# Low parts of the context stream's weight pieces: from GpSimd to VectorE

## Chip, cores and metric

The kernel runs on one core of one Trainium2 chip. The metric is device time in microseconds (us) of one launch. A core has five engines that run side by side, each through its own instructions in a fixed order: TensorE (PE, with weight loads as PEld), VectorE (DVE), ScalarE (ACT), GpSimd (POOL) and SyncE (SP, which here only issues DMAs).

## The reference

Two blocks follow each other. The first runs on 256 tokens of x: two token mixers side by side, then a gated FFN. One of the mixers is a recurrence over the tokens. The second block has two layers on x and on 256 context tokens: half FFNs, three mixers, and shifts, scales and gates that come from a large product with `w_ada`. All data are float32.

```
def first_block(x, ...):
    xn = rms_norm(h, norm_mix[l])
    proj = xn @ w_in[l]
    y_r = rwkv7_group(proj[..., :R_COLS], ...)
    y_n = nsa_group(proj[..., R_COLS:], ...)
    h = h + jnp.concatenate([y_r, y_n], axis=-1) @ w_out[l]
    h = h + swiglu(rms_norm(h, norm_ffn[l]), ...)
# in rwkv7_group, one step per token:
    sa = jnp.einsum('bhvk,bhk->bhv', state, an_t)
    state = state * w_t[:, :, None, :] + sa[..., None] * b_t[:, :, None, :] + v_t[..., None] * k_t[:, :, None, :]
# second block
def _half_ffn(h, g, shift, scale, gate, w_up, w_down):
    return h + 0.5 * gate * _swiglu(_modulate(_rmsnorm(h, g), shift, scale), w_up, w_down)
mod_x = (jax.nn.silu(c) @ w_ada[l] + b_ada[l]).reshape(bn, 1, N_MOD, d)
h_c = _half_ffn(h_c, norm_g[l, 0], mod_c[:, :, 0], mod_c[:, :, 1], mod_c[:, :, 2], ffn1_up[l], ffn1_down[l])
```

## The kernel before

A float32 matrix product is made of three matmuls in a reduced float32 format. Weights and activations are each split into a high part, which is the value rounded to that format, and a low part, which is the rest. `gemm` (lines 360 to 366) runs high by high (line 364), low activation by high weight (365), and high activation by low weight (366). A weight piece of 128 x 1024 elements is brought by one DMA of 512 KB (line 349). ScalarE rounds it to its high part (line 356), and then another engine subtracts that from the piece, which leaves the low part (line 357). Such a piece feeds 24 matmuls of 256 columns.

`Stream` holds the buffers of such pieces and the engine that subtracts, `self.e`. There are three streams. `s1` and `s` carry the weights of x and subtract on VectorE. `sc` carries the weights of the context (the words "context stream" below) and is made with `eng=g`, so that its subtractions run on GpSimd. It has three buffers for raw pieces and two each for high and low parts. Through it go the 66 pieces of the context's first half FFN (44 up, 22 down) and the 14 pieces of the context's projections in layer 0, 80 in all; pieces of `w_ada` pass its raw buffers without a split.

The program is written as a sequence of pieces, and a scheduler decides in which order each engine's instructions stand; what an instruction is thought to take is the scheduler's own estimate. So a change of the engine for one kind of instruction can move others. Every engine then runs its list in order.

Around the change the first block and the context's first half FFN run interleaved. The first block's tile names on PE and DVE are those of block1: `P`, `sm` and `nm` are its attention, `lw`, `cum`, `kk`, `rk` the start of the recurrence (from line 823). Then come the Gram products (line 946), and a triangular solve in 31 steps on VectorE (`tm` and `TW`, lines 972 and 973), whose result goes through DRAM and back by DMAs (lines 975 and 979) into `TT`. The scan over 8 chunks follows: lines 989 to 1002 prepare it, and a chunk is line 1018 on PE, 1019 on DVE (`U`), 1021, 1026 and 1027 on PE, 1036 on DVE (`SB`), with 1035 on POOL. Its end goes over a norm with a power on POOL (line 850) to the last products 1078 and 1079. After that PE takes the first block's output projection (tile `m`, line 364 with `mixh`) and its FFN. The context FFN's matmuls have tiles `f` with `yhc`, `ylc` (up) and `hh`, `hl` (down); line 1163 are the `w_ada` matmuls. The context's next norm sums squares on POOL (line 398, tile `sa`), then on PE (388), and spreads its factor by line 421.

Of the kernel before, what the change touches and what calls it, by code (L numbers as in the profile page):

```python
# [15 lines left out]
OP = mybir.AluOpType  # L16
# [249 lines left out]
def build(tc, A, O, dbg=(), stop=None):  # L266
    nc = tc.nc
    v, s, g, te, sy = nc.vector, nc.scalar, nc.gpsimd, nc.tensor, nc.sync
    es = ExitStack()

    def pool(name, bufs=1, space=None, side=None, stack=es, **k):
        if space is not None:
            k["space"] = space
        if side is not None:
            k["side"] = side
        return stack.enter_context(tc.tile_pool(name=name, bufs=bufs, **k))
# [7 lines left out]
    def tl(p, shape, dt=F32, tag="", bufs=None, name=None):  # L284
        k = {}
        if tag:
            k["tag"] = tag
        if bufs:
            k["bufs"] = bufs
        return p.tile(list(shape), dt, name=uniq(name or tag or "t"), **k)  # L290
# [8 lines left out]
    f32 = lambda a: a.bitcast(F32)  # L299
# [31 lines left out]


    class Stream:
        def __init__(self, name, nr, nh, side=None, stack=es, eng=None, parts=None):
            self.nr = nr
            self.raw = pool(name + "r", nr, side=side, stack=stack)
            self.h = pool(name + "h", nh, side=side, stack=parts or stack)
            self.l = pool(name + "l", nh, side=side, stack=parts or stack)
            self.q = sy
            self.e = eng or v  # L340

        def load(self, src, a, b, i=0):

# [8 lines left out]
        def get(self, src, a, b):  # L352
            r = self.load(src, a, b)
            h = tl(self.h, [128, 1024], F32R, tag="h")[:, 0:a * b].rearrange("p (a b) -> p a b", a=a)
            l = tl(self.l, [128, 1024], F32R, tag="l")[:, 0:a * b].rearrange("p (a b) -> p a b", a=a)
            s.copy(h, r)  # L356
            self.e.tensor_tensor(l, r, f32(h), op=OP.subtract)  # L357
            return h, l

    def gemm(pt, w, m0, m1, xs):  # L360
# [1218 lines left out]
    R = "right"  # L1579
# [4 lines left out]

    rs, rs2 = ExitStack(), ExitStack()
    pad = pool("pada", 1, side=R, stack=rs)
    st_c = Stream("sc", 3, 2, side=R, stack=rs, eng=g, parts=rs2)
    st_c.pad = pad
    e = ExitStack()
    first = []  # L1590
# [89 lines left out]
    rs = ExitStack()  # L1680
# [75 lines left out]
```

## Time and profile before

| | before |
|---|---|
| median of 3 runs | 2326.54 us (2321.26 to 2328.99) |
| the profiled execution's own time | 2326.68 us |
| its span, first to last instruction | 2324.7 us |
| mean granted TensorE clock | 0.977 |
| PE busy | 2226.8 us, 96% of the span |
| PEld busy | 1943.0 us, 84% |
| DVE busy | 1367.7 us, 59% |
| ACT busy | 944.8 us, 41% |
| POOL busy | 367.5 us, 16% |

The span is the time between the first and the last instruction of that execution; the run's own time is some 2 us longer. PE's busy time is made of matmuls whose ends overlap, so a busy PE may still be waiting between small matmuls. The granted clock is the share of 2.4 GHz that TensorE got: it is either 1.0 or 0.5 at any moment, and a row shows its mean.

### The profile page before, as it was taken

To read this page: it belongs to the slowest core of one execution; us is meant where nothing else is said; L and a number is where in the kernel's file an instruction comes from. 1 tells how busy PE (TensorE), PEld (TensorE's weight loads), DVE (VectorE), ACT (ScalarE), POOL (GpSimd) and SP (SyncE) were. 2 spreads that over 40 slices of the span, in tenths; PEclk is the share of its full clock that TensorE was granted. 3 is DMA by queue.
4 is the path that set the end of the run, shared out by engine and by line. 5 is a ranking of instruction groups with operands and counts; after the bars stand their busy time and mean duration, and the time that the engine had idled before them with its cause. 6 is when DMAs were issued, how large, how long until landed. Compare 5 with 4: busy or idle time off the path is not lost.

```text
span 2324.7 us, 38368 instructions
## 1 busy us (share of the span) xinstructions
PE 2226.8 (96%) x15317; PEld 1943.0 (84%) x15317; DVE 1367.7 (59%) x2442; ACT 944.8 (41%) x1602; POOL 367.5 (16%) x286
## 2 busy tenths in 40 slices
PE   7999987999999899998999999999999999999998
PEld 3688876888999799997878777789988889878998
DVE  4555567348665776677765333357534347885665
ACT  4334431225444454445643222235322225574443
POOL 2124543455110300002010000011000001410000
PEclk9999988999999899999999999999999999999999
DMA  7865434336554234544166434465522234413553
GB/s 294 277 231 182 176 135 139 124 118 243 191 182 172 100 127 167 183 172 145 55 227 227 161 129 162 146 227 199 200 97 95 96 110 166 150 57 114 187 184 129
DMA packets 114929, 376.25 MB, mean 162 GB/s; under 512 B 18464, under 2 KB 24480, under 8 KB 114752
## 3 DMA queue, kind: packets, MB, share of 16 engines
q1 hardware_dynamic: 114752, 373.82, 46.4%
q8 instruction: 120, 1.97, 0.3%
q14 instruction: 57, 0.47, 0.1%
HBM read 372.20 MB, written 1.57 MB: 161 GB/s over the span
## 4 chain that ended last, share of the span: by engine, by line
PE 76%; issue 11%; DVE 7%; DMA 3%; POOL 2%; ACT 1%; SPq 0%; POOLq 0%; DVEq 0%; ACTq 0%
PE m L364 13%; PE m L366 13%; PE m L365 13%; PE f L364 7%; PE f L366 7%; PE f L365 7%; PE f L1163 4%; PE o L1391 2%; POOL sa L398 1%; DMA r<-in_ada 1%; PE f L1381 1%; DVE l L357 1%; DVE tm L972 1%; ACT h L356 1%; DMA r<-in_up 1%
## 5 line engine op out<-in xcount | busy, mean ns | idle before, releaser
L356 ACT CAST h<-r 128x1024 fp32r<-128x1024 f32 (+1 forms) x547 | 567.0, 1042 | 1050.3 <-PE m L365 426.2
L357 DVE TENSOR_TENSOR l<-r,h 128x1024 fp32r<-128x1024 f32 (+1 forms) x467 | 572.0, 1228 | 351.8 <-ACT h L356 342.3
L364 PE MATMUL m<-yh,h 128*128 128x256 f32 (+1 forms) x1624 | 489.5, 303 | 2.3 <-ACT h L356 1.1
L366 PE MATMUL m<-yh,l 128*128 128x256 f32 (+1 forms) x1624 | 489.1, 302 | 0.4 <-DVE l L357 0.4
L365 PE MATMUL m<-yl,h 128*128 128x256 f32 (+1 forms) x1624 | 489.5, 302 | 0.0
L364 PEld LDWEIGHTS m<-yh,h 128*128 128x128 f32 x1624 | 310.0, 191 | 25.8 <-ACT h L356 8.9
L366 PEld LDWEIGHTS m<-yh,l 128*128 128x128 f32 x1624 | 310.4, 191 | 18.2 <-issue 7.1
L365 PEld LDWEIGHTS m<-yl,h 128*128 128x128 f32 x1624 | 310.6, 191 | 15.4 <-issue 3.7
L357 POOL TENSOR_TENSOR l<-r,h 128x1024 fp32r<-128x1024 f32 x80 | 193.4, 2419 | 335.2 <-ACT h L356 327.7
L398 POOL TENSOR_TENSOR sa<-sa,sq 128x256 f32<-128x256 f32 x81 | 86.2, 1064 | 907.3 <-ACT sq L394 490.0
L365 PE MATMUL m<-hl,h 128*128 128x256 f32 (+1 forms) x738 | 220.1, 302 | 0.0
L366 PE MATMUL m<-hh,l 128*128 128x256 f32 (+1 forms) x738 | 219.9, 303 | 0.0
L364 PE MATMUL m<-hh,h 128*128 128x256 f32 (+1 forms) x738 | 215.5, 304 | 0.2
L364 PE MATMUL f<-yh,h 128*128 128x256 f32 (+1 forms) x624 | 199.6, 320 | 1.8 <-ACT yh L434 1.1
L365 PE MATMUL f<-yl,h 128*128 128x256 f32 (+1 forms) x624 | 198.0, 317 | 1.2 <-DVE yl L435 1.2
L366 PE MATMUL f<-yh,l 128*128 128x256 f32 (+1 forms) x624 | 197.9, 318 | 0.0
L364 PE MATMUL f<-hh,h 128*128 128x256 f32 (+1 forms) x446 | 138.5, 316 | 13.8 <-DVE ft L461 6.5
L366 PEld LDWEIGHTS m<-hh,l 128*128 128x128 f32 x738 | 139.1, 189 | 8.4 <-issue 1.6
L365 PEld LDWEIGHTS m<-hl,h 128*128 128x128 f32 x738 | 139.8, 190 | 6.7 <-issue 0.4
L364 PEld LDWEIGHTS m<-hh,h 128*128 128x128 f32 x738 | 136.3, 189 | 10.0 <-issue 2.1
L1541 DVE SCALAR_TENSOR_TENSOR res<-m,mod,res 128x256 f32<-128x256 f32 x176 | 79.1, 478 | 105.5 <-PE m L366 105.0
L365 PE MATMUL f<-hl,h 128*128 128x256 f32 (+1 forms) x446 | 136.8, 309 | 0.3 <-DVE hl L370 0.3
(513 smaller groups left out, 4079.6 us busy)
## 6 DMA issues: line engine op xcount, KB each, us to landing
r<-in_up SPq DMA_DIRECT2D x252, 512.0 KB, 3.6
r<-in_ada SPq DMA_DIRECT2D x144, 512.0 KB, 4.4
r<-in_dn SPq DMA_DIRECT2D x98, 512.0 KB, 3.8
r<-in_w1u SPq DMA_DIRECT2D x44, 512.0 KB, 3.5
r<-in_dn SPq DMA_DIRECT2D x32, 448.0 KB, 3.3
r<-in_w2m SPq DMA_DIRECT2D x24, 512.0 KB, 4.1
r<-in_w2o SPq DMA_DIRECT2D x24, 512.0 KB, 3.5
r<-in_w1d SPq DMA_DIRECT2D x22, 512.0 KB, 3.5
```

What stands on the lines that cost most here:

```text
L356: s.copy(h, r)
L357: self.e.tensor_tensor(l, r, f32(h), op=OP.subtract)
L364: te.matmul(pt, w[0][:, k, m0:m1], xs[k][0], start=k == 0, stop=False)
L365: te.matmul(pt, w[0][:, k, m0:m1], xs[k][1], start=False, stop=False)
L366: te.matmul(pt, w[1][:, k, m0:m1], xs[k][0], start=False, stop=k == n - 1)
L398: g.tensor_tensor(acc, acc, sq, op=OP.add)
L972: v.tensor_mul(tm, TW[:, 0:m, j:j + 1].to_broadcast([128, m, n]), Ls[:, j:j + 1, j + 1:32].to_broadcast([128, m, n]))
L1163: te.matmul(pt[j * 32:j * 32 + 32], adac[:, k], w[j], start=k == 0, stop=k == KD - 1)
L1381: te.transpose(pT[:, b * 128:b * 128 + 128], P[:, b * 128:b * 128 + 128], ident)
L1391: te.matmul(po[j * 64:j * 64 + 64], vals(b // 2, b % 2, kvof(2 * pr + j)), PT[j][:, b], start=b == 0, stop=b == nt - 1)
L1541: v.scalar_tensor_tensor(r, pt[:, i * T:i * T + T], ad[l].M[:, m, d, q:q + 1], r, op0=OP.mult, op1=OP.add)
```

## The change

The subtraction for the context stream's pieces goes to VectorE, with the same operands. The choice of an engine is taken out of `Stream`.

```diff
     class Stream:
-        def __init__(self, name, nr, nh, side=None, stack=es, eng=None, parts=None):
+        def __init__(self, name, nr, nh, side=None, stack=es, parts=None):
             self.nr = nr
             self.raw = pool(name + "r", nr, side=side, stack=stack)
             self.h = pool(name + "h", nh, side=side, stack=parts or stack)
             self.l = pool(name + "l", nh, side=side, stack=parts or stack)
             self.q = sy
-            self.e = eng or v
...
             s.copy(h, r)
-            self.e.tensor_tensor(l, r, f32(h), op=OP.subtract)
+            v.tensor_sub(l, r, f32(h))
             return h, l
...
-    st_c = Stream("sc", 3, 2, side=R, stack=rs, eng=g, parts=rs2)
+    st_c = Stream("sc", 3, 2, side=R, stack=rs, parts=rs2)
```

The file is one line shorter above line 356, so that a line of before is one lower in the changed kernel (356 is 355, 357 is 356, and so on). The scheduler puts the engines' lists into another order. Three places follow. Numbers behind the tiles' names tell buffers apart.

First PE, in the scan over chunks: the rows of one chunk from line 1018 on, and what stands behind its first product of line 1026. Tiles `f` are the context FFN. Before:

```order
L1018 MATMUL m_2514<-SB_406_1913,WT_2290 32x128 x4
L1021 MATMUL o_2463<-AR_2009,SB_406_1913 128x32 x4
L1026 MATMUL m_2524<-Vt_2078,Kt_2064 128x128
L364 MATMUL f_4895<-hh_4562,h_4877 128x256
L365 MATMUL f_4895<-hl_4563,h_4877 128x256
L366 MATMUL f_4895<-hh_4562,l_4878 128x256
```

Now:

```order
L1017 MATMUL m_2489<-SB_407_1914,WT_2290 32x128 x4
L1020 MATMUL o_2463<-AR_2009,SB_407_1914 128x32 x4
L1025 MATMUL m_2499<-Vt_2078,Kt_2064 128x128
L1026 MATMUL m_2499<-U_2334,Bt_2050 128x128
L1025 MATMUL m_2499<-Vt_2078,Kt_2064 128x128
L1026 MATMUL m_2499<-U_2334,Bt_2050 128x128
```

The context FFN's matmuls, 14 of them at this place, are gone from between the first product and the one that reads `U`; in the changed order none stands anywhere in the scan.

Second PE, at the end of the recurrence, around its last products. Before:

```order
L364 MATMUL f_5143<-hh_5011,h_5139 128x256
L1078 MATMUL m_2629<-gl_29_144,lora_2609 128x256
L1079 MATMUL m_2629<-gl_30_145,lora_2611 128x256
L1078 MATMUL m_2635<-gl_29_144,lora_2609 128x256
L1079 MATMUL m_2635<-gl_30_145,lora_2611 128x256
L365 MATMUL f_5143<-hl_5012,h_5139 128x256
```

Now:

```order
L1077 MATMUL m_2635<-gl_29_144,lora_2609 128x256
L1078 MATMUL m_2635<-gl_30_145,lora_2611 128x256
L387 MATMUL f_8025<-ones_67,sa_8026 128x1 x2
L420 MATMUL f_8056<-sq_8053,ones_67 128x256
L363 MATMUL m_5260<-mixh_147,h_5256 128x256
L364 MATMUL m_5260<-mixl_148,h_5256 128x256
L363 MATMUL f_8104<-yhc_8019,h_8100 128x256
```

The context FFN was still running there; now it is over, and the sums of the context's next norm (387 and 420) stand between the recurrence and the output projection.

Third DVE, in the triangular solve. Before:

```order
L972 TENSOR_TENSOR tm_2247<-TW_2181,Ls_2178 128x11x11
L973 TENSOR_TENSOR TW_2181<-TW_2181,tm_2247 128x11x11
L972 TENSOR_TENSOR tm_2250<-TW_2181,Ls_2178 128x11x10
L973 TENSOR_TENSOR TW_2181<-TW_2181,tm_2250 128x11x10
L972 TENSOR_TENSOR tm_2253<-TW_2181,Ls_2178 128x12x9
```

Now, with the pieces' low parts among the steps:

```order
L971 TENSOR_TENSOR tm_2205<-TW_2181,Ls_2178 128x4x25
L356 TENSOR_TENSOR l_4738<-r_4735,h_4737 128x1024
L972 TENSOR_TENSOR TW_2181<-TW_2181,tm_2205 128x4x25
L369 TENSOR_TENSOR hl_4720<-ft_4717,hh_4719 128x256
L971 TENSOR_TENSOR tm_2208<-TW_2181,Ls_2178 128x4x24
L972 TENSOR_TENSOR TW_2181<-TW_2181,tm_2208 128x4x24
L971 TENSOR_TENSOR tm_2211<-TW_2181,Ls_2178 128x5x23
L972 TENSOR_TENSOR TW_2181<-TW_2181,tm_2211 128x5x23
L356 TENSOR_TENSOR l_4810<-r_4807,h_4809 128x1024
```

The subtractions stand inside the chain that each next step reads.

## Rows read from the trace of the kernel before

**Rows 1.** The cores' view: span and mean granted clock.

```profile
core 0: 2324.7 us, clock 0.977
```

**Rows 2.** Windows: stretch, length, busy us (and instructions) per engine, clock, DMA share, GB/s.

```profile
118.00:287.80 169.80, 164.97 (x1303) 136.38 (x1302) 92.73 (x214) 72.40 (x160) 70.75 (x35) 0.99 0.54 193
287.80:363.30 75.50, 68.66 (x417) 53.64 (x416) 47.57 (x84) 20.71 (x31) 34.69 (x16) 0.91 0.42 143
363.30:414.10 50.80, 37.31 (x256) 32.52 (x255) 36.11 (x82) 11.67 (x15) 21.32 (x9) 0.87 0.45 138
414.10:522.50 108.40, 106.88 (x847) 92.33 (x846) 43.40 (x69) 25.98 (x40) 47.97 (x32) 0.97 0.34 119
522.50:569.00 46.50, 43.44 (x332) 39.08 (x332) 39.50 (x81) 26.13 (x44) 26.43 (x25) 0.96 0.80 278
793.00:814.00 21.00, 13.24 (x48) 10.86 (x48) 14.84 (x41) 9.48 (x25) 8.71 (x11) 0.51 0.07 26
2150.00:2200.00 50.00, 50.00 (x427) 50.00 (x426) 32.53 (x49) 21.62 (x28) 0.00 (x0) 1.00 0.53 182
```

**Rows 3.** Costliest groups of the page, line 357: busy, mean ns, idle before and releaser.

```profile
L357 DVE TENSOR_TENSOR l<-r,h 128x1024 fp32r<-128x1024 f32 (+1 forms) x467 | 572.0, 1228 | 351.8 <-ACT h L356 342.3
L357 POOL TENSOR_TENSOR l<-r,h 128x1024 fp32r<-128x1024 f32 x80 | 193.4, 2419 | 335.2 <-ACT h L356 327.7
```

**Rows 4.** Timeline of DVE in the solve: start us, us taken, instruction.

```profile
366.14 0.19 DVE L972 TENSOR_TENSOR tm<-TW,Ls 128x31 f32<-128x31 f32 x1 [1.85 <-DMA TW<-in_cst]
...
373.14 0.28 DVE L973 TENSOR_TENSOR TW<-TW,tm 128x115 f32<-128x115 f32 x1
373.46 2.43 DVE L972 TENSOR_TENSOR tm<-TW,Ls 128x110 f32<-128x110 f32 x1
...
403.69 0.19 DVE L973 TENSOR_TENSOR TW<-TW,tm 128x16 f32<-128x16 f32 x1
```

**Rows 5.** Timeline of POOL at the same time.

```profile
373.41 2.35 POOL L357 TENSOR_TENSOR l<-r,h 128x1024 fp32r<-128x1024 f32 x1 [4.60 <-ACT h L356]
```

**Rows 6.** Groups by line from 128 to 569 us.

```profile
L370 DVE TENSOR_TENSOR hl<-ft,hh 128x256 fp32r<-128x256 f32 x22 | 33.3, 1513 | 7.6 <-ACT hh L369 7.5
L398 POOL TENSOR_TENSOR sa<-sa,sq 128x256 f32<-128x256 f32 x14 | 14.7, 1053 | 15.6 <-ACT sq L394 14.6 <-DMA pw<-in_poolw 0.6
```

**Rows 7.** Waits of PE from 118 to 414 us: total, times, longest.

```profile
PE f L364 <- DVE ft L461: 6.5, 1, 6.5
PE f L364 <- DVE res L1541: 5.1, 4, 3.3
PE m L886 <- DVE rk L882: 4.3, 1, 4.3
...
PE f L364 <- DVE fu L457: 1.8, 1, 1.8
```

**Rows 8.** Timeline of PE in one chunk of the scan (filler left out).

```profile
442.38 1.04 PE L1018 MATMUL m<-SB,WT 128*32 128x128 f32 x8
443.34 1.08 PE L1021 MATMUL o<-AR,SB 128*128 128x32 f32 x8
444.35 0.48 PE L1026 MATMUL m<-Vt,Kt 32*128 32x128 f32 x2
...
446.87 0.48 PE L1027 MATMUL m<-U,Bt 32*128 32x128 f32 x2
...
448.31 0.38 PE L1027 MATMUL m<-U,Bt 32*128 32x128 f32 x2
```

**Rows 9.** Timeline of DVE in the same chunk.

```profile
443.45 0.69 DVE L1019 TENSOR_TENSOR U<-m,Uv 32x512 f32<-32x512 f32 x1 [2.79 <-PE m L1018]
...
448.80 0.87 DVE L1036 TENSOR_TENSOR SB<-st,m 64x256 f32<-64x256 f32 x2 [4.21 <-PE m L1027]
```

**Rows 10.** Timeline of PE: the same eight transposes (line 859) at either clock level.

```profile
314.85 1.09 PE L859 MATMUL m<-cst,rx 128*128 128x128 f32 x8
...
513.56 1.94 PE L859 MATMUL m<-cst,rx 128*128 128x128 f32 x8 [1.10 <-DVE rx L854]
```

## The prediction

> **What bounds the kernel now.** I start from the cores' view: one span of 2324.7 us at a mean clock of 0.977 [rows 1]. The profiled execution took 2326.68 us, against which I make the sum; the median of the runs is 2326.54 us, so the two can be read as one. PE is the bound, with 96% of the span busy. The change can therefore pay only where PE waits, and cost only where it makes PE wait.
>
> Next I cut the time in which the context stream's pieces are used into stages, by what PE has in its list [rows 2]. Stage A (118 to 287.8 us) is the first block's attention with context FFN between, B (to 363.3) the start of the recurrence, C (to 414.1) the triangular solve and its way through DRAM, D (to 522.5) the scan and its end, E (to 569) the output projection. On PE they end at the first matmul of line 823, the last of 946, the first of 989, the last of 1079, and the first of the first block's FFN. From there on the lists of before and after agree again but for small shifts. The reader should see two things in these rows. PE is less busy in B and C than elsewhere (68.66 of 75.5 us, 37.31 of 50.8), and the clock is lower there, 0.91 and 0.87. In D it is busy for 106.88 of 108.4 us, because context FFN fills its gaps.
>
> Then I look at what PE waits for in A to C [rows 7]: the four DVE waits shown make 6.5 + 5.1 + 4.3 + 1.8 = 17.7 us. DVE is not full there, 36.11 of 50.8 us in C. Its timeline says why it is late: a step of the solve takes 0.28 us, and the next like it 2.43 us [rows 4], just while POOL subtracts for 2.35 us [rows 5]. This instruction, which reads two operands from SBUF, stands through the whole POOL subtraction. The group of line 370 shows the same: 256 columns take 1513 ns on average [rows 6], longer than 1228 ns for the 1024 columns of a low part on DVE [rows 3].
>
> **The change part by part.** It removes 80 subtractions of 2419 ns from POOL and adds 80 of about 1228 ns to DVE [rows 3]: 80 x 1.228 = 98 us of DVE work. On the other side DVE no longer stands still beside POOL. From line 370 alone that is at least 22 x (1.513 - 0.69) = 18 us, since 512 columns take 0.69 us in a like instruction [rows 9]; if every one of the 80 stopped DVE as in rows 4, it would be 80 x 2.15 = 172 us. DVE is busy for about 0.4 of D (43.40 of 108.4 us [rows 2]), so I take 0.4 x 172 = 69 us, and DVE's net load grows by 29 us only. Where PE is full without the recurrence, as in the plain FFN stage with DVE at 32.53 of 50 us [rows 2], the rest of the 80 hides; there I cost it at nothing, bounded by 2 us either way.
>
> What matters more is the order. Counting rows of the two lists, context FFN matmuls move forward on PE: A has 866 split matmuls before and 1104 now (of the first block's projection and the context FFN together), B 252 and 287, C 225 and 337, D 362 and none, E 311 and 288. Of the small `w_ada` matmuls, 34 leave D and E for A and C. A split matmul costs 50 us / 427 = 0.117 us when PE is full [rows 2].
>
> A to C: 385 x 0.117 = 45.0 us more PE work, and 34 x 0.117 = 4.0 us as an estimate for the small ones, 49 us in all. Against it stands what was lost there: 17.7 us of DVE waits, and by the clock 169.8 x 0.01 + 75.5 x 0.09 + 50.8 x 0.13 = 15 us. I count two thirds of the waits (12 us) and a third of the clock's loss (5 us) as recovered, because subtractions now stand inside the solve on DVE: 31 steps in 37.7 us before [rows 4], now with 13 pieces between them (13 x 1.23 = 16 us), while the stalls of that stretch go. So D begins 49 - 17 = 32 us later. Bounds: nothing recovered, +49; all, +16.
>
> On DVE a subtraction waits for its ScalarE cast, which waits until PE frees a buffer; on POOL such waits, 327.7 us in all [rows 3], held up little. On DVE the solve and the attention's steps queue behind them, and PE waits for those. That is why I don't count everything as recovered. The SP queue now issues the solve's DMAs behind later weight pieces, at about the point where PE reaches them; I cost that at nothing, hidden by C's filler.
>
> D: its filler is gone. Taking 362 + 28 - 6 matmuls at 0.117 us out of 108.4 us leaves 63 us, if the clock stays as it was (0.97) and nothing that lay hidden comes to light. One chunk then takes 0.96 + 1.01 + 0.48 us on PE up to the product that reads `U` (the DVE add of 0.69 us fits beside it [rows 9]), 1.93 us to DVE's start and 0.87 us there: 5.25 us [rows 8, 9], of which PE has 4.38. But PE now has gaps in each chunk. Where it had such gaps, from 793 to 814 us, the granted clock was 0.51 [rows 2], that is, the level of 1.2 GHz nearly all the time. The same eight transposes take 1.09 us at the upper level and 1.94 at the lower, 1.78 times as long [rows 10]. At that level a chunk costs 4.38 x 0.78 = 3.4 us more, six chunks 20.5, and the head and tail about 10 by the same factor on an estimated 13 us: D would take 94 us. I take the middle, 81 us, with a little towards the lower clock: D gets 27 us shorter. Bounds: 45 and 14 us shorter.
>
> The Trainium skill bears on this in "TensorE: Matmul & The Clock Gate", section "HAM oscillation": short bursts of matmuls with waits between them drop the array to half rate again and again. By that page D would sit at its upper bound throughout, and the sum would come out 13 us higher than mine. In this trace the stretch at 0.51 agrees with it; the scan with filler between, in a stage at 0.97, could not show it.
>
> E: 23 split and 12 small matmuls fewer, 4 us. But the context's next norm now stands in PE's list between the recurrence and the projection. Its seven adds on POOL of 1.05 us [rows 6] queue behind the power of line 850, and PE waits for them and then for the factor. I take 6 us for that, so E is 2 us longer; bounds 0 and +8.
>
> Sum: +32 - 27 + 2 = +7 us, so 2326.7 + 7 = 2333.7, that is **2334 us**. The outermost ends would be 16 - 45 + 0 = -29 and 49 - 14 + 8 = +43.
>
> **The rivals.** First, faster: the scan holds the upper clock. Then D is 45 us shorter, and the sum 32 - 45 + 2 = -11, so 2316 us. For it speaks that PE waits for only 0.87 us of a chunk's 5.25, and for 21 - 13.24 = 7.8 us of the 21 us in the stretch at 0.51. It decides where less than about a seventh of D runs at the lower clock: 0.14 x 31 us is what separates it from a gain of 7 us. Against it speaks that B and C, with gaps and filler, already fell to 0.91 and 0.87 [rows 2].
>
> Second, slower by more: D stays at the lower clock from end to end, 32 - 14 + 2 = +20, so 2347 us. The page on the clock gate in the Trainium skill, named above, would have it so. For it speaks 0.51 in rows 2; against it, that the matmuls get longer there and leave smaller gaps.
>
> Third, no difference: what leaves D fills what was lost in A to C, and the time agrees within 0.3%, 2320 to 2333 us. It needs a recovery of some 24 us rather than 17, or a D of 75 us. For it speaks that DVE has room by its share and that the stalls [rows 4, 6] are the very waits of rows 7.
>
> That the change does nothing can be set aside: 80 instructions are gone from POOL's list and stand on DVE's.
>
> **How the numbers follow.** My forecast, a loss of 3 to 14 us, has a chance of 0.35; of this, 0.25 lies beyond 0.3%, which is 7 us and about what a measurement of this kernel tells from no change. The half-clock rival has 0.25, all slower. No difference has 0.20, and 0.10 comes from the lower part of the forecast. The faster rival has 0.20. So faster 0.20, same 0.30, slower 0.50. The range takes in the faster rival and most of the half-clock one: 2316 to 2352 us; of the outermost ends about 1 in 10 is left out on each side. As cases of both signs are in it, the likeliest case alone spans 2330 to 2341 us.
>
> **What would show it.** In the changed profile, no DVE step of the solve should take 2.4 us, and line 370 should fall towards half a microsecond. Line 357's group on POOL should be gone, and DVE's busy time should be about 1400 us. The first line 988 (989 of before) should start near 446 us. A chunk of the scan should take between 5.25 and 8.7 us with no tile `f` in it, the clock there lying between 0.5 and 1. PE should wait for `sa` and for the DVE factor before the projection, and the first product of the first block's FFN should come near 576 us. I am wrong in the mechanism if the scan still takes about 10 us per chunk, if the waits of rows 7 grow, or if the difference arises after 576 us.

## The result, and the profile after

The changed kernel takes 2356.13 us in the median of 4 runs (2351.56 to 2357.05), beside 2327.76 us for the kernel before (2321.26 to 2329.58, 4 runs): a ratio of 1.0123 with a 95% interval of 1.0099 to 1.0147. It is slower by 28 us; 2334 was forecast, and 2352 was the upper end of the range. The profiled execution is the fastest of the four, 2351.56 us with a span of 2348.6, so the two traces show 23.9 us of the difference.

The page of the changed kernel, busy time by engine, and the line of the subtraction, which is now 356 ([rows 3] before). Line numbers of the changed kernel are one lower than before:

```profile
PE 2243.8 (96%) x15317; PEld 1956.0 (83%) x15317; DVE 1393.8 (59%) x2522; ACT 945.2 (40%) x1602; POOL 176.1 (7%) x206
...
L356 DVE TENSOR_TENSOR l<-r,h 128x1024 fp32r<-128x1024 f32 (+1 forms) x547 | 670.6, 1229 | 419.7 <-ACT h L355 406.0
```

All 547 subtractions are on DVE at 1229 ns, POOL lost its 80, and DVE's busy time grew by 26 us only. PE, with the same 15317 matmuls, is busy for 17 us longer.

The windows by stage tell where (columns as in [rows 2]; stages A, B, C, D, then E up to the first product of the first block's FFN, then the scan's part of D alone, then all that follows E):

```profile
118.00:316.40 198.40, 195.94 (x1544) 163.01 (x1542) 121.41 (x266) 80.27 (x170) 1.37 (x5) 1.00 0.58 202
316.40:393.90 77.50, 71.43 (x458) 54.87 (x456) 55.53 (x101) 25.82 (x38) 9.58 (x5) 1.00 0.43 146
393.90:447.70 53.80, 49.43 (x407) 42.62 (x408) 41.88 (x110) 15.81 (x22) 0.00 (x0) 1.00 0.65 209
447.70:542.10 94.40, 79.31 (x441) 64.64 (x441) 24.36 (x39) 9.46 (x17) 16.23 (x20) 0.66 0.13 46
542.10:587.40 45.30, 39.62 (x301) 38.53 (x302) 36.83 (x84) 25.18 (x43) 12.49 (x15) 0.89 0.57 195
464.30:519.70 55.40, 49.79 (x242) 42.91 (x242) 11.54 (x21) 0.58 (x1) 7.69 (x12) 0.53 0.06 20
587.40:2348.60 1761.20, 1708.66 (x11626) 1529.73 (x11624) 1054.82 (x1800) 740.83 (x1231) 120.79 (x124) 0.98 0.44 151
```

The same views of the kernel before, from the first product of the first block's FFN on, and of its scan:

```profile
571.20:2324.70 1753.50, 1704.48 (x11626) 1525.72 (x11624) 1048.94 (x1791) 739.80 (x1229) 143.47 (x134) 0.98 0.44 152
432.40:490.70 58.30, 58.30 (x476) 51.35 (x477) 22.91 (x36) 11.59 (x15) 27.27 (x20) 1.00 0.32 112
```

Against [rows 2], D starts at 447.7 instead of 414.1 us (33.6 later), ends at 542.1 instead of 522.5 (19.6 later), E ends 16.2 us later, and the rest is 7.7 us longer. For the end of E these figures take the first product of the first block's FFN as the trace of before has it, at 571.2 us; at the 569.0 us of [rows 2], matmuls of the context (tile `f`) still run:

```profile
571.19 0.51 PE L364 MATMUL m<-yh,h 128*128 128x256 f32 x3
```

The reader should see three things. A to C now run at a clock of 1.00, where B and C had 0.91 and 0.87. The scan has about half as many matmuls (242 for 476), and yet takes nearly as long, 55.4 for 58.3 us: its clock fell from 1.00 to 0.53. Ahead of the scan and behind it, D kept more of the clock, 0.95 and 0.75 (see the two lines below). And the waits of [rows 7] have gone, as the waits of PE from 118 to 447 us show (total, times, longest; the three largest):

```profile
PE f L363 <- ACT h L355: 3.4, 2, 2.3
PE f L365 <- DVE l L356: 2.8, 4, 0.8
PE f L1162 <- DMA r<-in_ada: 2.1, 3, 1.2
```

D of the changed kernel ahead of the scan and behind it (windows as above; in the kernel before the same two parts take 18.3 and 31.8 us):

```profile
447.70:464.30 16.60, 14.65 (x125) 11.60 (x126) 3.93 (x7) 4.23 (x6) 0.56 (x1) 0.95 0.56 197
519.70:542.10 22.40, 14.87 (x78) 10.13 (x77) 8.89 (x12) 4.65 (x10) 7.98 (x8) 0.75 0.00 1
```

DVE no longer stands beside POOL either. The group of [rows 6], line 370 and now 369, from 128 to 588 us:

```profile
L369 DVE TENSOR_TENSOR hl<-ft,hh 128x256 fp32r<-128x256 f32 x22 | 9.2, 419 | 2.5 <-ACT hh L368 2.5
```

That is 419 ns where it was 1513. A chunk of the scan, by DVE's timeline (start, us taken; compare [rows 9]), lasts 483.31 - 474.75 = 8.56 us:

```profile
474.75 0.69 DVE L1018 TENSOR_TENSOR U<-m,Uv 32x512 f32<-32x512 f32 x1 [2.07 <-PE m L1017]
480.37 0.87 DVE L1035 TENSOR_TENSOR SB<-st,m 64x256 f32<-64x256 f32 x2 [4.93 <-PE m L1026]
483.31 0.70 DVE L1018 TENSOR_TENSOR U<-m,Uv 32x512 f32<-32x512 f32 x1 [2.07 <-PE m L1017]
```

In D, the largest waits of PE are its own chain's, and then, in E, that for the factor of the context's next norm:

```profile
PE m L1017 <- DVE SB L1035: 5.6, 5, 1.1
PE m L858 <- DVE rx L853: 4.1, 1, 4.1
PE f L420 <- DVE sq L418: 3.9, 1, 3.9
```

### The profile page after: what moved, and what is told of

It is laid out like the page before. It is cut to its first block, busy times and chain, and to the rows that moved or that the text cites. A ratio compares the mean times of both kernels' runs of the same rounds, so it can differ in the third digit from the quotient of the medians.

```text
span 2348.6 us, 38357 instructions
## 1 busy us (share of the span) xinstructions
PE 2243.8 (96%) x15317; PEld 1956.0 (83%) x15317; DVE 1393.8 (59%) x2522; ACT 945.2 (40%) x1602; POOL 176.1 (7%) x206
## 3 DMA queue, kind: packets, MB, share of 16 engines
q1 hardware_dynamic: 114752, 373.82, 45.9%
## 4 chain that ended last, share of the span: by engine, by line
PE 78%; issue 10%; DVE 5%; DMA 3%; ACT 2%; POOL 2%; SPq 0%; POOLq 0%; DVEq 0%; ACTq 0%
PE m L363 13%; PE m L365 13%; PE m L364 13%; PE f L363 7%; PE f L365 7%; PE f L364 7%; PE f L1162 3%; PE o L1390 2%; DVE l L356 1%; POOL sa L397 1%; ACT h L355 1%; PE f L1380 1%; DMA r<-in_up 1%; DMA r<-in_ada 1%; DMA r<-in_dn 1%
## 5 line engine op out<-in xcount | busy, mean ns | idle before, releaser
L356 DVE TENSOR_TENSOR l<-r,h 128x1024 fp32r<-128x1024 f32 (+1 forms) x547 | 670.6, 1229 | 419.7 <-ACT h L355 406.0
L365 PE MATMUL f<-hh,l 128*128 128x256 f32 (+1 forms) x446 | 133.0, 303 | 0.6 <-DVE l L356 0.6
```

Source lines behind the costliest of these rows:

```text
L356: v.tensor_sub(l, r, f32(h))
L365: te.matmul(pt, w[1][:, k, m0:m1], xs[k][0], start=False, stop=k == n - 1)
```

## The experiments

Theory 1 says that the loss is the order: the filler (context FFN matmuls) left the scan, and TensorE fell to the lower clock there. Theory 2 says that it is the engine: 80 more subtractions in DVE's queue hold up what PE waits for. Theory 3, against the clock's part in theory 1, says that a scan without filler is as long as its chain over DVE and POOL.

### Holding filler back by stages

The first way to give the scan its filler back was an edge in PE's list: the context FFN's groups 4 and 5 (432 split matmuls) may not stand ahead of the scan's preparation. Run on both engines:

```diff
+                    mark.append(te.matmul(pz[:, h * 64:h * 64 + 64], AK[t][:, h], ...))
...
+            with (tc.issue_after(mark[0].ins) if gi >= 4 else ExitStack()):
+                f.group(gi, st_c, pp, hp, psf, ...)
```

> The changed kernel (subtractions on VectorE), with the matmuls of the context FFN's last 18 pieces (groups 4 and 5, 432 split matmuls) queued on PE behind the first matmul that prepares the scan, so that the scan gets its filler back. Theory 1, the order: the change lost because the filler left the scan and the scan then ran at the lower clock. Then the scan's stage starts between 395 and 420 us (447.7 in the changed kernel), has a granted clock of 0.95 or more (0.66 there), and the whole takes 2310 to 2330 us, no slower than before. Theory 2, the engine: 80 more subtractions on VectorE hold up the recurrence and attention, which share its queue. Then the scan's stage still starts after 430 us although 50 us of filler are gone ahead of it, and the whole takes 2345 us or more.

> The same hold in the kernel before (subtractions on GpSimd). The order was already much like this, so both theories expect 2318 to 2335 us. What counts is the difference to the run with the hold and VectorE. Theory 1, the order: with like orders VectorE is the better engine, by up to the 17.7 us of DVE waits and the clock lost beside GpSimd's subtractions, so this run is 5 to 20 us slower than that one. Theory 2, the engine: this run is faster than that one by 10 us or more.

Measured: on VectorE 2339.80 us (ratio 1.0068, 1.0049 to 1.0088), on GpSimd 2344.94 (1.0092, 1.0071 to 1.0113). D did start early on VectorE, at 410.0 us, but all filler ahead of the edge was used up in A and B. PE's windows with the hold on VectorE, for C and for the head of D:

```profile
380.70:410.00 29.30, 0.00 (x0) 0.01 (x1) 17.24 (x67) 0.00 (x0) 0.00 (x0) 0.54 0.21 41
410.00:437.90 27.90, 27.88 (x142) 26.64 (x143) 2.64 (x5) 3.31 (x6) 1.24 (x2) 0.51 0.03 5
```

PE had nothing at all in C, and behind that hole it ran at half clock for the 27.9 us of the head, although it was never idle there. Neither theory had this. The run on GpSimd came out 5.1 us behind that on VectorE, which speaks against theory 2 and lies at the lower edge of what theory 1 expected; but the lists of the two were not alike, and neither theory is decided by it.

Three runs then held the filler at the start of B, of C and of D, in different shares (the edge is chosen for each product `pa`, `pb`, `pd` of the FFN, by its number; the numbers shown are those of the first run, and `mark` holds the matmuls at which D, C and B begin):

```diff
+        def held(n):
+            gate.close()
+            for a, k in ((66, 'D'), (53, 'C'), (38, 'B')):
+                if n_[0] >= a:
+                    gate.enter_context(tc.issue_after(mark[k].ins))
+                    break
+            n_[0] += 1
+            return psf(n)
```

> The changed kernel, subtractions on VectorE, with the context FFN's split matmuls held behind the recurrence's own stages so that PE's list has nearly the counts of the kernel before: 720, 264, 216 and 384 of the FFN's 1584 in stages A, B, C and from D on (before: 722, 252, 225 and 385). Theory 1, the order: what was lost came from the filler's place, and VectorE is otherwise no worse. Then A to C takes no longer than before (D starts at 405 to 416 us), D 104 to 112 us at a clock of 0.94 or more, and the whole 2308 to 2328 us. Theory 2, the engine: 80 subtractions more on VectorE hold up its chains, and PE's waits in A to C grow. Then D starts after 420 us and the whole takes 2335 us or more.

> The same with 768, 287, 289 and 240 of them, between before and the changed kernel (960, 287, 337, 0). Theory 1: D starts at 418 to 426 us and, with 214 of them in the scan, takes 82 to 92 us at a clock of 0.9 or more; the whole 2310 to 2330 us. Theory 2, the engine: nothing gained over the changed kernel but the clock, 2338 us or more.

> The same with 864, 288, 288 and 144 of them. It tells how much filler the scan needs. Theory 1, the clock: 138 in the scan fill its gaps only in part; if that holds the clock, D takes 72 to 82 us and the whole 2315 to 2330 us, if not 90 to 100 us and 2340 us or more. Theory 2, the engine: as for the run before, 2338 us or more.

Measured: 2350.36 us (1.0106, 1.0072 to 1.0141), 2355.14 (1.0134, 1.0100 to 1.0168) and 2352.01 (1.0116, 1.0085 to 1.0147). By the totals theory 2 seemed to hold: the first has nearly the counts of before in every stage and still loses 27 us. Its trace says otherwise. Waits of PE from 118 to 418 us, and the windows of A, of C and of the head of D:

```profile
PE m L990 <- DMA TT<-d_t: 14.3, 1, 14.3
PE m L773 <- DVE P L766: 4.0, 3, 1.9
```

```profile
118.00:299.20 181.20, 167.08 (x1285) 137.31 (x1284) 105.85 (x242) 70.64 (x158) 1.36 (x5) 0.96 0.53 186
371.10:417.70 46.60, 30.88 (x244) 27.07 (x244) 33.11 (x94) 11.91 (x16) 0.00 (x0) 0.87 0.59 188
417.70:444.80 27.10, 27.07 (x141) 25.89 (x141) 2.64 (x5) 2.86 (x5) 1.24 (x2) 0.52 0.03 4
```

PE is idle for 14.1 of 181.2 us in A and 15.7 of 46.6 in C, and the wait for a subtraction is not among the largest two. The 14.3 us are the wait for the solve's result (line 990 here is 989 of before) after the stage's filler had run out. The head of D then ran at 0.52. The other two show the same: behind waits of 12.4 and 11.5 us for the solve's result, their heads took 26.9 and 28.0 us at 0.50, with PE never idle there. Behind an edge the filler comes as soon as it may, and the end of the stage is bare; equal counts per stage are not an equal order. So these runs could not part the theories, and a finer one was needed.

The other two tell what the scan needs. Its windows in these two runs follow. By their traces, 211 split matmuls of the context FFN and 32 of `w_ada` stand in the first, 116 and 56 in the second (not 138: 29 of the 144 that were held to D stand in its head):

```profile
457.60:516.70 59.10, 59.10 (x485) 52.24 (x486) 28.89 (x48) 10.52 (x14) 6.18 (x10) 1.00 0.32 108
```

```profile
462.10:518.20 56.10, 55.15 (x416) 43.79 (x415) 22.86 (x42) 7.38 (x11) 6.17 (x10) 0.93 0.37 128
```

With 116 and 56 the clock held 0.93, and the scan took 56.1 us, hardly more than the 55.4 us of the changed kernel with none: there, filler for 116 x 0.117 = 14 us of PE, and the `w_ada` matmuls beside it, were nearly free. Yet neither run was faster than the changed kernel: D starts earlier there, at 430.7 and 434.1 us, but takes 116.9 and 110.7 us, as its head is 10 and 11 us longer than the 16.6 us of the changed kernel, and its tail too is longer.

### The whole list of PE, on either engine

The scheduler can be given edges that fix the order on one engine. With one edge for each pair of neighbours, PE's whole list of one kernel was laid on the other:

```diff
+    traced = {i.name: i for i in nc.cur_bb.bb.instructions}
+    for a, b in zip(ids, ids[1:]):
+        tc.add_manual_dep(traced[f"I-{b}"], f"I-{a}", mybir.DependencyInfo(mybir.DependencyClass.NoSync, mybir.DependencyReason.DATA))
```

`ids` are the 14415 matmuls and transposes in the other kernel's order.

> The changed kernel, all 80 subtractions on VectorE, but PE's whole list pinned, instruction by instruction, to that of the kernel before (14415 matmuls and transposes in the same order). Only the engine of the subtraction and the orders on the other engines that follow from it differ from before. Theory 1, the order: the loss comes from where the filler stands in PE's list. Then the loss is gone, and what VectorE saves beside GpSimd (up to the 17.7 us of PE's waits for VectorE in A to C) comes out: 2305 to 2326 us, PE's idle time in A to C at most the 25 us of before. Theory 2, the engine: the subtractions stand in VectorE's queue ahead of what PE waits for. Then PE's idle time in A to C grows with the same list, and the whole takes 2340 us or more.

> The other way round: the kernel before, all 80 subtractions on GpSimd, with PE's whole list pinned to that of the changed kernel. Theory 1, the order: it is as slow as the changed kernel or slower, 2350 to 2385 us, with the scan at half clock. Theory 2, the engine: 2320 to 2335 us, as before, although the scan has no filler.

Medians in us, with the ratio to before and its interval:

| PE's list | low parts on GpSimd | low parts on VectorE |
|---|---|---|
| of before | 2322.76 (before itself, here) | 2321.25; 0.9994 (0.9982 to 1.0006) |
| of the changed kernel | 2393.56; 1.0297 (1.0280 to 1.0314) | 2356.13; 1.0123 (1.0099 to 1.0147), against 2327.76 |

With the list of before, the engine makes no difference that can be measured; with the engine of either kernel, the new list is slower. Theory 2 has fallen, and the loss is that of PE's order. (Only PE's list is pinned; those of the other engines may differ between the runs.) That the subtraction sits on VectorE is even a help with the new list, by 1.0297 / 1.0123, or 1.7%. There GpSimd's subtractions do the harm that was forecast. DVE's groups from 118 to 492 us, GpSimd and the new list, then VectorE and the old list:

```profile
L370 DVE TENSOR_TENSOR hl<-ft,hh 128x256 fp32r<-128x256 f32 x22 | 26.0, 1181 | 18.2 <-ACT hh L369 18.2
...
L972 DVE TENSOR_TENSOR tm<-TW,Ls 128x126 f32<-128x126 f32 (+22 forms) x31 | 18.0, 581 | 0.8
```

```profile
L370 DVE TENSOR_TENSOR hl<-ft,hh 128x256 fp32r<-128x256 f32 x20 | 8.4, 418 | 0.5 <-ACT hh L369 0.5
...
L972 DVE TENSOR_TENSOR tm<-TW,Ls 128x126 f32<-128x126 f32 (+22 forms) x31 | 7.9, 253 | 4.4 <-DMA TW<-in_cst 3.7
```

The same two operations take 1181 and 581 ns beside GpSimd, 418 and 253 without it. The Trainium skill says in "SBUF — State Buffer", section "Who interferes with whom", that these two engines share one pair of ports, which one locks for itself; the trace agrees, with these numbers.

Why then is nothing gained with the old list? C, D and the head of D, VectorE and the list of before, and what PE waits for longest:

```profile
350.00:397.70 47.70, 32.73 (x254) 28.40 (x253) 31.45 (x91) 12.62 (x16) 0.00 (x0) 0.91 0.53 172
397.70:513.30 115.60, 115.34 (x847) 100.80 (x847) 50.45 (x84) 25.25 (x40) 12.65 (x16) 0.89 0.30 102
397.70:424.60 26.90, 26.86 (x153) 25.43 (x154) 5.36 (x9) 4.08 (x7) 1.23 (x2) 0.60 0.08 24
```

```profile
PE m L989 <- DMA TT<-d_t: 11.3, 1, 11.3
```

D starts at 397.7 us, 16.4 us earlier than in [rows 2]. Of this, only 2.9 us are idle time of PE, 22.2 us in A to C where it was 25.2: the waits of [rows 7] are gone, but one wait of 11.3 us has come in their place. The other 13.5 us are busy time, 257.5 us where it was 270.9, with clocks of 1.00, 0.98 and 0.91 in A, B and C where they were 0.99, 0.91 and 0.87 (19 matmuls fewer fall into the stretch, some 2 us by 0.117 us each). Behind the one wait PE runs at 0.60 through the head of D, and D is 7.2 us longer than in [rows 2]. In this execution 9.8 us of span are left as a gain; it lies 4 us below the median of its own runs, and the medians show no difference.

### One part of the change

The kernel before, with the 14 projection pieces on VectorE and the 66 pieces of the FFN on GpSimd:

```diff
         mixc = mix_tiles()
+        st_c.e = v
         mixer(0, "c", st_c, ...)
```

> The kernel before with one part of the change: the 14 pieces of the context's projections on VectorE, the 66 of its FFN still on GpSimd. The order up to the end of the recurrence is that of before. Theories 1 and 2 put the loss into the FFN's pieces and expect the time of before within 0.3% (2318 to 2332 us), D at 414 us. If the projections carry the loss, 2340 us or more.

Measured: 2329.39 us, 1.0022 (1.0000 to 1.0044). The projections carry at most 0.44% of the 1.23%; the rest of the loss comes with the FFN's pieces.

### The clock in the scan

To the changed kernel, extra matmuls were added at the end of a chunk, 6 or 16; they read constants and overwrite a product that has been read:

```diff
+                        for _ in range(16 if c else 0):
+                            tc.keep_in_program_order(te.matmul(pu[:, 0:256], causb[:, 0], causb.rearrange("p a b -> p (a b)"), start=True, stop=True))
```

> The changed kernel with 6 extra bfloat16 matmuls of 256 columns at the end of each of the chunks 1 to 6 of the scan (36 in all; they read constants and write to the chunk's product that has been read, so nothing else changes). Theory 1, the clock: the scan loses because TensorE runs at half clock in it. The extra matmuls (36 x 0.11 = 4 us at the upper clock, mostly inside the wait for the next SB) lift the clock, a chunk falls from 8.4 to below 7 us, the stage from 94 us to 70 to 85, and the whole to 2327 to 2342 us. Theory 3, latency: a chunk's length is set by the chain over DVE and POOL, the clock follows from it. Then the stage stays at 92 us or more and the whole at 2349 us or more.

> As before with 16 extra matmuls per chunk (96 in all, 10 to 20 us of PE work). Theory 1, the clock: the clock in the scan is near 1.0, a chunk takes 5.25 us and some 1 us for what of the extra matmuls its gap does not hold, the stage 72 to 82 us, the whole 2330 to 2340 us. Theory 3, latency: the extra matmuls only lengthen the chunk, the stage takes 98 us or more and the whole 2355 us or more.

Measured: 2350.44 us (1.0107, 1.0082 to 1.0132) and 2343.06 (1.0087, 1.0063 to 1.0111). The windows of the scan with 6 and then with 16, against the 55.4 us at 0.53 of the changed kernel:

```profile
465.20:518.30 53.10, 52.33 (x278) 42.74 (x279) 11.62 (x21) 0.59 (x1) 7.80 (x12) 0.60 0.06 20
```

```profile
466.10:514.60 48.50, 48.45 (x338) 39.85 (x340) 11.53 (x21) 0.58 (x1) 7.78 (x12) 0.80 0.07 23
```

Sixteen more per chunk make the scan 6.9 us shorter, although they are 96 matmuls more on the same engine. D with 16:

```profile
449.50:539.60 90.10, 80.51 (x537) 62.00 (x537) 26.54 (x45) 10.60 (x20) 16.23 (x20) 0.79 0.14 49
```

That is 90.1 us where theory 3 expected 98 or more and the changed kernel has 94.4. But 6 per chunk did next to nothing (0.60, and 96.1 us for D), which is what theory 3 expected of that run, and even 16 lifted the clock to 0.80 only: theory 1 had expected more of both. So it is the run with 16 alone that speaks against theory 3, by the windows of one execution; the whole times of these runs and of the changed kernel have intervals that overlap.

### Filling the wait ahead of the scan

On VectorE with the list of before, 96 split matmuls of the FFN were moved to the end of C, into the wait of 11.3 us, from the end of D and E. The only edit to the kernel above is the order of `ids`; it was run on both engines.

> The subtractions on VectorE, PE's list pinned to that of the kernel before but for one move: 96 split matmuls of the context FFN more stand at the end of the solve's stage, just ahead of the first matmul that prepares the scan, and 96 fewer at the end of D and in E. With the list of before and VectorE, PE waited there 11.3 us for the solve's result and then ran 21.7 us at half clock. 96 x 0.117 = 11.2 us fill that wait. Theory 1, the order: the wait goes, the clock holds in the head of the scan (10.8 us of it), and the whole falls by 15 to 22 us against the run with the list of before, to 2299 to 2308 us. Rival: the filler itself waits there for its pieces, or delays the scan by as much as it fills, and the whole stays within 2315 to 2326 us.

> The same list with the subtractions on GpSimd. If VectorE is the better engine at any list, PE waits beside GpSimd's subtractions in A to C as before (25 us idle there), and this run is 10 us or more slower than the one on VectorE, 2315 to 2335 us. If the engine does not matter once the list is given, both agree within 0.4%.

Measured: 2341.25 us (1.0060, 1.0042 to 1.0079) and 2351.29 (1.0096, 1.0076 to 1.0117). VectorE is 10 us better at this list, but the list is worse than that of before, which neither theory 1 nor its rival had expected. C, D and the head of D on VectorE, and PE's longest wait from 118 to 420 us:

```profile
349.10:402.80 53.70, 44.52 (x350) 40.01 (x350) 37.78 (x101) 17.13 (x23) 0.00 (x0) 0.99 0.55 182
402.80:530.20 127.40, 118.30 (x774) 99.99 (x775) 48.81 (x81) 23.05 (x37) 15.39 (x20) 0.79 0.24 80
402.80:433.20 30.40, 30.39 (x152) 28.71 (x152) 4.86 (x9) 4.17 (x7) 1.23 (x2) 0.51 0.13 39
```

```profile
PE m L989 <- DMA TT<-d_t: 5.8, 1, 5.8
```

A wait of 5.8 us remained. The solve got longer, 42.6 us from its first step to its last where it was 36.1 with the list of before, with ten more DVE instructions in C (101 for 91). Behind that wait the head again ran at half clock, and the end of D had lost its filler: PE is idle for 9.1 us of D, where it was 0.3.

The last run fills the wait with work that displaces nothing: 96 extra matmuls on constants, ahead of the first matmul of line 989, on VectorE with the list of before.

```diff
+                for _ in range(96 if t == 0 else 0):
+                    te.matmul(pw[:, 0:256], causb[:, 0], causb.rearrange("p a b -> p (a b)"), start=True, stop=True)
```

> The subtractions on VectorE and PE's list pinned to that of before, with 96 extra bfloat16 matmuls of 256 columns just ahead of the first matmul that prepares the scan, where PE otherwise waits 11.3 us for the solve's result and then runs 21.7 us at half clock. They read constants and write to the product that the next matmul begins anew, so no other work moves. 96 x 0.107 = 10.3 us of the wait is filled. If the clock alone makes the loss behind a gap, the head of the scan (26.8 us) falls to 16 to 20 us, D from 115.6 to 104 to 109 us, and the whole is 2308 to 2316 us, faster than both kernels. If the time behind the gap is set by what the head waits for, D stays at 113 us or more and the whole at 2318 to 2330 us.

Measured: 2308.88 us (2305.38 to 2314.07), a ratio of 0.9940 (0.9923 to 0.9956): faster than both kernels. D and its head:

```profile
399.10:503.60 104.50, 103.95 (x847) 89.81 (x848) 50.39 (x85) 25.31 (x40) 12.73 (x16) 1.00 0.33 113
399.10:416.30 17.20, 16.87 (x152) 15.87 (x152) 5.10 (x9) 4.08 (x7) 1.24 (x2) 1.00 0.13 38
```

The head takes 17.2 us at 1.00, where it took 26.9 at 0.60; D is 11.1 us shorter. The 96 extra matmuls cost 1.4 us, by which D starts later. What the wait had cost the head of D was the clock, and with it held, a gain comes out. How much of this gain is VectorE's is not shown, as the same filling was not run with the subtractions on GpSimd; in the kernel before, D already ran at 0.97, so by the prediction's formula for the clock some 108.4 x 0.03 = 3 us stood to be won in it (an estimate), and 16 us were won.

## Why the prediction was wrong

The direction was right, and so was the mechanism in the main, order and clock. The forecast, 2334 us, was 22 us too low against the median and 17.6 us against the profiled execution. Its terms, one by one, against the trace of the changed kernel:

- **A to C, +32: measured +33.6.** The sum held, its two parts were both too small. PE is busy for 45.9 us more in the three stages (316.8 instead of 270.9) though the clock's loss, 15 us by the prediction's formula, has gone; so the work moved in is some 61 us by that estimate, not 49. (The kernel on VectorE with the list of before gives 316.8 - 257.5 = 59 us, 57 without the 19 matmuls that it counts fewer.) Recovered were, by the same estimate, all of the clock's 15 us, and 12.3 us of idle time (25.2 to 12.9 us): 27 and not 17. That the sum came out is thus in part luck. The doubt about DVE's queue was not needed: the solve does get longer with the pieces' low parts in it, 41.1 us from its first step to its last for 37.7, but PE has filler meanwhile.
- **D, -27: measured -14.0.** This is the step that failed: "I take the middle, 81 us". D took 94.4, the bound that the prediction had worked out for half clock from end to end. In the scan this bound was right for its own reason: a chunk takes 8.56 us from one `U` to the next (bounds 5.25 and 8.7), and the clock is 0.53. In the head and the tail it was not: they ran at 0.95 and 0.75, and D's mean is 0.66. That all of D agrees with the bound to 0.4 us is in part luck. No row had spoken for the middle: 0.51 in the one stretch with like gaps [rows 2] was the nearest, and 0.97 was that of a scan with filler. The half-clock rival, 2347, was the likeliest by that row, and had 0.25.
- **E, +2: measured -3.4** (16.2 - 19.6). The wait for the factor of the context's norm is there, 3.9 us where 6 were taken for it and `sa`, but the stage was shorter all the same. The prediction had also ended E of before at 569.0 us, 2.2 us ahead of the product that it names.
- **After E, 0: measured +7.7**, 1753.5 to 1761.2 us, of which 4.2 us are PE's busy time at the same count of matmuls and 3.5 its waits. The prediction had put this term at nothing, within 2 us. Its cause stays open. It looks as if it went with the list: before, its list on VectorE and that with the wait filled take 1750.6 to 1753.5 us there, the changed kernel and the one on GpSimd pinned to its list 1761.2 and 1761.4. But the two runs with 96 matmuls moved, which share one list of PE, take 1758.5 on VectorE and 1752.7 on GpSimd, so a difference of this size does not need another list. Each figure is of one execution.

33.6 - 14.0 - 3.4 + 7.7 = 23.9 us, the difference of the spans. Had D been put at its upper bound, the forecast would have been +20 us, 2347; the 3.9 us left are +1.6 from A to C, -5.4 from E and +7.7 from after E. The median of the four runs lies another 4.6 us above the profiled execution, which these traces can't explain.

The rule of the Trainium skill that was weighed, "TensorE: Matmul & The Clock Gate", section "HAM oscillation", would have D at its upper bound throughout; the trace agrees in the scan, with a clock of 0.53, and not in the head and the tail of D, with 0.95 and 0.75. The page describes waits longer than the bursts between them, while PE is idle for 5.6 of the scan's 55.4 us only, so what agrees is the outcome. The rival that D holds the upper clock fell by the same rows; 211 split matmuls in the scan, with 32 of `w_ada`, were enough to hold 1.00, as one of the runs showed.

Of the signs, no step of the solve takes 2.4 us any more (0.30 at most), line 370 fell to 419 ns, DVE's busy time is 1393.8 us, the first matmul of line 988 came at 447.7 us (446 forecast), and most of the difference, 16.2 of 23.9 us, arises before the first block's FFN. Wrong were the time of that FFN's first product, 587.4 us for 576 (578 from its true place before), and the wait for `sa`, which PE does not have: it waits for the factor alone.

## What to carry to other kernels

A change of engine can be a change of order: where a scheduler lays the lists, first fix the order of the engine that bounds the kernel, and measure the engine and the order apart, as the table of two by two does. Filler that can run early is worth most where PE has short waits in a chain; a list that used it up before made the chain run at half clock here, and equal counts per stage did not help where a stage ended bare. A single wait of PE is priced with what runs behind it, and filling it with matmuls on constants may pay for itself, as it did here once.

## What was not expected of the hardware

A wait can cost more than its length. Behind one of 11.3 us PE ran the next 26.9 us at 0.60, behind 5.8 us the next 30.4 us at 0.51, and behind 29.3 us the next 27.9 us at 0.51; in all three it was idle for less than 0.1 us of those stretches. The three runs that held the filler by stages show the same, 0.50 to 0.52 over 26.9 to 28.0 us behind 11.5 to 14.3 us. With the wait filled, 152 matmuls of the same stretch ran at 1.00 and took 17.2 us. A PE that the profile shows as full may thus run at the lower clock: the column of the granted clock has to be read beside it.
